# An attention-score kernel: transposes over other PSUM buffers, evacuation two to one, and another place for the second unit's transposes

## The chip, the core and the metric

The kernel runs on one core of one Trainium2 chip. The metric is the device time of one execution in microseconds. Three runs of the kernel before gave 202.73, 202.91 and 203.09; the median is 202.91.

## The reference

```
batch, heads, seq, dim = 8, 8, 512, 64          # q and k, float32
scale = 1.0 / np.sqrt(q.shape[-1])
out = (np.einsum('bhqd,bhkd->bhqk', q, k) * scale).astype(np.float32)
```

For each of 64 pairs of batch and head, a 512 by 64 matrix `q` is multiplied with the transpose of a `k` of the same size, and scaled by 1/8. There is no softmax. Inputs are 16.8 MB, the output is 67.1 MB.

## The kernel before, in words

**Units and tiles.** The eight batches are taken two at a time: four units (`v`). A unit's `k` and `q` are loaded as 128 partitions of 16 KB each, so a partition holds 64 consecutive rows of one head. A unit's output is written in four tiles (`t`), each of four heads of one batch: two pairs of heads (`x`), with eight rows (`i`) of 512 per partition. That is 128 by 8192 floats, 4 MiB, one DMA each. So there are 8 loads of 2 MiB and 16 stores of 4 MiB, all issued by SP, in one queue, in the order of the program.

**Buffers in SBUF.** `big_pool` has three buffers of 4 MiB, and both a unit's inputs and an output tile take one. Four units are loaded at the start of the program: units 0, 1 and 2 take the three buffers, unit 3 takes the first again as soon as unit 0 is cast. Output tile 0 takes the buffer of unit 1, tile 1 that of unit 2, tile 2 that of unit 3, tile 3 that of tile 0, and so on: a tile's buffer is free when the store three before it has landed.

**Casts.** `load_and_cast` (L73) turns each input into bf16 `xb` in two halves, on POOL (L82).

**Transposes.** `transpose` (L98) is a generator. TensorE transposes eight 128 by 128 blocks into one PSUM bank (`tp`, two buffers; L107 for `k`, L116 for `q`), and `rearrange` (L87) copies the bank to SBUF in four copies of 64 partitions (L95), into `kT` or into `qz`, which holds zeros between its halves. Whole tiles alternate between DVE and ACT by the counter `n_tp`. A unit has four such tiles of `k` and four of `q`, and each tile gives five steps of the generator: its transposes, then four copies.

**Scores and evacuation.** `scores` (L123) multiplies into `ps` (three buffers of two banks, L132) and `evacuate` (L60) scales 128 by 1024 floats from PSUM to the output tile: 8 per tile, 128 in all. Of each six, three are on ACT (L64) and three on DVE (L66).

**Order.** All of these are pinned to the program's order on their engine. Unit 0 is transposed at once. From then on the steps of the next unit's generator are taken between evacuations of the present unit (L158): one or two after each.

Of the kernel before, what the change touches and what calls it, by code (L numbers as in the profile page):

```python
# [1 line left out]

# [5 lines left out]


@with_exitstack  # L10
def kernel(
    ctx: ExitStack,
    tc: tile.TileContext,
    q: bass.AP,
    k: bass.AP,
    out: bass.AP,
):

    nc = tc.nc
    B, H, S, D = q.shape
    scale = 1.0 / (D ** 0.5)
    P = 128
    UNITS = B // 2
    N = H
    M = P // (2 * H)  # L30
    R = S // M
    J = R // 2
    RO = 8
    U = S // RO
    JJ = J // RO
    IW = 8 // JJ
    TILES = N // 2

    f32 = mybir.dt.float32
    bf16 = mybir.dt.bfloat16  # L40

    q_r = q.rearrange("(v b) g (m j) d -> v (b g m) (j d)", b=2, j=R)
    k_r = k.rearrange("(v b) g (m j) d -> v (b g m) (j d)", b=2, j=R)
    out_r = out.rearrange("(v b) (t x h) (u i) k -> v (b t) (h u) x (i k)", b=2, x=2, h=2, i=RO)

    consts = ctx.enter_context(tc.tile_pool(name="consts", bufs=1))

    big_pool = ctx.enter_context(tc.tile_pool(name="big", bufs=3))
    bf_pool = ctx.enter_context(tc.tile_pool(name="bf", bufs=6))
    t_pool = ctx.enter_context(tc.tile_pool(name="t", bufs=2))  # L50
    tpsum_pool = ctx.enter_context(tc.tile_pool(name="tpsum", bufs=2, space=bass.MemoryType.PSUM))
    psum_pool = ctx.enter_context(tc.tile_pool(name="psum", bufs=3, space=bass.MemoryType.PSUM))


    pinned = tc.keep_in_program_order

    n_evac = 0
    n_tp = 0

    def evacuate(dst, src):  # L60
        nonlocal n_evac

        if n_evac % 6 in (0, 2, 3):
            pinned(nc.scalar.mul(out=dst, in_=src, mul=scale))  # L64
        else:
            pinned(nc.vector.tensor_scalar(out=dst, in0=src, scalar1=scale, scalar2=None,  # L66
                                           op0=mybir.AluOpType.mult))
        n_evac += 1

    def half(h):  # L70
        return slice(h * D, (h + 1) * D)

    def load_and_cast(v):  # L73

        xf = big_pool.tile([P, 2, 2, J * D], f32, name="big")
        both = []
        for x, src in enumerate((k_r, q_r)):
            nc.sync.dma_start(out=xf[:, x], in_=src[v].rearrange("p (s c) -> p s c", s=2))  # L78
        for x in range(2):
            xb = bf_pool.tile([P, J, 2, D], bf16, name="xb")  # L80
            for s in range(2):
                pinned(nc.gpsimd.tensor_copy(out=xb[:, :, s, :],  # L82
                                             in_=xf[:, x, s].rearrange("p (j d) -> p j d", j=J)))
            both.append(xb)
        return both

    def rearrange(tp, pattern, dst):  # L87

        nonlocal n_tp
        copy = (nc.vector.tensor_copy, nc.scalar.copy)[n_tp % 2]  # L90
        n_tp += 1
        for s in range(2):
            src = tp[half(s)].rearrange(pattern, n=N, h=2)
            for h in range(2):
                pinned(copy(out=dst(s, h), in_=src[:, h]))  # L95
                yield

    def transpose(v, kb, qb):  # L98


        kT = t_pool.tile([P, N, M, 2, J], bf16, name="kT")
        qz = qzs[v % 2]
        ts[v] = (kT, qz)
        for j0 in range(0, J, 8):
            tp = tpsum_pool.tile([P, 8, P], bf16, name="tp")
            for j in range(8):
                pinned(nc.tensor.transpose(out=tp[:, j, :], identity=identity,  # L107
                                           in_=kb[:, j0 + j].rearrange("p s d -> p (s d)")))
            yield
            yield from rearrange(tp, "d j (n h m) -> d h n m j",  # L110
                                 lambda s, h: kT[half(h), :, :, s, j0:j0 + 8])
        for i0 in range(0, RO, IW):
            tp = tpsum_pool.tile([P, IW, JJ, P], bf16, name="tp")
            for i in range(IW):
                for jj in range(JJ):
                    pinned(nc.tensor.transpose(out=tp[:, i, jj, :], identity=identity,  # L116
                                               in_=qb[:, RO * jj + i0 + i].rearrange("p s d -> p (s d)")))
            yield
            yield from rearrange(tp, "d i jj (n h m) -> d h i n m jj",
                                 lambda s, h: qz[half(h), i0:i0 + IW, :, h * U:(h + 1) * U]  # L120
                                 .rearrange("d i n (m s jj) -> d s i n m jj", s=2, jj=JJ)[:, s])

    def scores(v, t):  # L123

        kT, qz = ts[v]
        o = big_pool.tile([P, 2, RO, S], f32, name="big")
        for x in range(2):
            n = 2 * t + x
            for i in range(0, RO, 2):
                ps = psum_pool.tile([P, 2, S], f32, name="ps")  # L130
                for w in range(2):
                    pinned(nc.tensor.matmul(out=ps[:, w, :], lhsT=qz[:, i + w, n, :],  # L132
                                            rhs=kT[:, n].rearrange("d m s j -> d (m s j)"),
                                            start=True, stop=True))
                evacuate(o[:, x, i:i + 2, :], ps)
                yield
        nc.sync.dma_start(out=out_r[v, t], in_=o.rearrange("p x i k -> p x (i k)"))  # L137

    def take(steps, count):
        for _ in range(count):  # L140
            next(steps, None)

    identity = consts.tile([P, P], dtype=bf16)
    make_identity(nc, identity)
    qzs = [consts.tile([P, RO, N, P], bf16, name=f"qz{n}") for n in range(2)]
    for qz in qzs:
        nc.vector.memset(qz, 0.0)  # L147
    cast = [load_and_cast(v) for v in range(UNITS)]

    ts = {}  # L150
    for _ in transpose(0, *cast[0]):
        pass
    for v in range(UNITS):
        ahead = transpose(v + 1, *cast[v + 1]) if v + 1 < UNITS else iter(())
        for t in range(TILES):
            for n, _ in enumerate(scores(v, t)):

                take(ahead, 1 + (t > 0 if v == 0 else n % 4 == 3))  # L158
        for _ in ahead:
            pass  # L160


# [1 line left out]
_INS = ['q', 'k']  # L164
_OUTS = [((8, 8, 512, 512), 'float32')]


# [23 lines left out]
```

## Time and profile before

| | |
|---|---|
| median of three runs | 202.91 us |
| the profiled execution | 203.03 us |
| its span, first to last instruction | 201.3 us |
| busy: PE, DVE, ACT, POOL | 99.2, 126.4, 100.7, 30.6 us |
| queue q1 (all loads and stores) | 83.89 MB, 98.1% of 16 engines |
| mean granted TensorE clock | 0.833 |

The span lies within the profiled execution's time, with 1.7 us around it. The page gives busy time by engine, then the span in 40 slices of 5.03 us with a digit for the busy tenths of each engine and of the DMA engines. A group of instructions is shown as busy time and mean duration, and then as the idle time of its engine just before them with what ended it. The windows view gives the same for stretches that one chooses, the timeline gives single instructions.

### The profile page before, as it was taken

How to read it: one execution, taken by the hardware profiler on the slowest of the kernel's cores; microseconds unless marked ns; L12 is line 12 of the kernel's file. 1: busy time of each engine (PE TensorE's matmuls, PEld its weight loads, DVE VectorE, ACT ScalarE, POOL GpSimd, SP SyncE). 2: the span in 40 equal slices, each digit the busy share in tenths (PEclk: the TensorE clock that was granted, in tenths of full speed). 3: DMA queues.
4: the chain of work that ended last, by engine and by line, in shares of the span. 5: the costliest groups of instructions: out<-in, count | busy, mean ns of one | idle time of the engine just before them, and what ended most of it. 6: DMA issues, size and time to landing. Idle time of an engine off the chain costs nothing.

```text
span 201.3 us, 1456 instructions
## 1 busy us (share of the span) xinstructions
PE 99.2 (49%) x503; PEld 48.3 (24%) x512; DVE 126.4 (63%) x130; ACT 100.7 (50%) x129; POOL 30.6 (15%) x22
## 2 busy tenths in 40 slices
PE   0033366753976729463729554856535666710000
PEld 0033353321522414231315221432212222200000
DVE  6726659995989929796749796569635264530000
ACT  2016667786674856583837663856515341510000
POOL 1277777556000000000000000000000000000000
PEclk9999999998599996999975998888995857555555
DMA  6999999999999999999999999999999999999993
GB/s 205 430 443 430 420 433 440 420 407 427 433 436 425 422 443 427 430 423 440 430 423 433 433 430 427 440 430 423 433 436 430 410 446 433 420 423 433 433 427 163
DMA packets 5510, 83.97 MB, mean 417 GB/s; under 512 B 384, under 2 KB 384, under 8 KB 384
## 3 DMA queue, kind: packets, MB, share of 16 engines
q1 hardware_dynamic: 5504, 83.89, 98.1%
q8 instruction: 4, 0.07, 0.1%
q14 instruction: 2, 0.02, 0.0%
HBM read 16.78 MB, written 67.11 MB: 417 GB/s over the span
## 4 chain that ended last, share of the span: by engine, by line
DMA 63%; DVE 16%; PE 3%; POOL 3%; ACT 1%; POOLq 1%; issue 1%; SPq 0%; DVEq 0%; ACTq 0%
DMA out_dram<-big 43%; DMA big<-in_q_dram 20%; DVE big L66 12%; PE ps L132 3%; DVE qz L95 3%; POOL xb L82 3%; DVE kT L95 1%; ACT big L64 1%; POOLq L186 1%; SPq L78 0%; DVEq L66 0%; SPq L137 0%; ACTq L64 0%; POOLq L82 0%
## 5 line engine op out<-in xcount | busy, mean ns | idle before, releaser
L132 PE MATMUL ps<-kT,qz 128*128 128x512 bf16 x247 | 81.1, 450 | 55.1 <-ACT big L64 39.2
L66 DVE TENSOR_SCALAR big<-ps 128x1024 f32<-128x1024 f32 x64 | 76.3, 1222 | 39.9 <-DMA out_dram<-big 29.1
L64 ACT ACTIVATE big<-ps 128x1024 f32<-128x1024 f32 x64 | 63.7, 1023 | 57.0 <-DMA out_dram<-big 30.8
L132 PEld LDWEIGHTS <-qz 128*128 128x128 bf16 x256 | 27.5, 111 | 96.0 <-issue 83.2
L82 POOL CAST xb<-big 128x2048 bf16<-128x2048 f32 x16 | 29.9, 1896 | 17.6 <-DMA big<-in_k_dram 11.9
L95 DVE COPY kT<-tp 64x512 bf16<-64x512 bf16 x32 | 22.0, 687 | 6.3 <-PE tp L107 5.7
L95 ACT COPY kT<-tp 64x512 bf16<-64x512 bf16 x32 | 18.5, 578 | 14.7 <-PE tp L107 14.4
L95 DVE COPY qz<-tp 64x512 bf16<-64x512 bf16 x32 | 22.0, 687 | 3.1 <-PE tp L116 2.7
L95 ACT COPY qz<-tp 64x512 bf16<-64x512 bf16 x32 | 18.5, 578 | 3.9 <-PE tp L116 3.6
L107 PE MATMUL tp<-identity,xb 128*128 128x128 bf16 x128 | 12.0, 254 | 16.5 <-POOL xb L82 12.5
L116 PE MATMUL tp<-identity,xb 128*128 128x128 bf16 x128 | 12.8, 265 | 6.0 <-DVE kT L95 3.5
L107 PEld LDWEIGHTS <-xb 128*128 128x128 bf16 x128 | 10.5, 116 | 20.8 <-POOL xb L82 12.8
L116 PEld LDWEIGHTS <-xb 128*128 128x128 bf16 x128 | 11.3, 122 | 10.9 <-issue 8.9
L147 DVE MEMSET qz<- 128x4096 uint32 x2 | 6.9, 3472 | 2.5 <-PEq L175 1.7
L95 ACT ACT_TABLE_LOAD x1 | 1.3, 1283 | 0.7 <-PEq L175 0.7
masks.py:199 POOL TENSOR_SCALAR_AFFINE_SELECT identity<-identity 128x128 bf16<-128x128 bf16 x1 | 0.3, 294 | 0.1
masks.py:197 POOL MEMSET identity<- 128x128 bf16 x1 | 0.2, 205 | 0.3 <-POOLq L175 0.3
L175 POOL MEMSET const-float32-0.0<- 128x1 f32 x1 | 0.1, 99 | 0.2 <-issue 0.2
L175 POOL MEMSET const-bfloat16-1.0<- 128x1 bf16 x1 | 0.1, 102 | 0.0
L175 POOL MEMSET const-uint8-127<- 128x1 uint8 x1 | 0.1, 102 | 0.0
L175 POOL MEMSET const-float32-1.0<- 128x1 f32 x1 | 0.1, 99 | 0.0
## 6 DMA issues: line engine op xcount, KB each, us to landing
out_dram<-big SPq DMA_DIRECT2D x16, 4096.0 KB, 21.4
big<-in_k_dram SPq DMA_DIRECT2D x4, 2048.0 KB, 19.2
big<-in_q_dram SPq DMA_DIRECT2D x4, 2048.0 KB, 24.2
```

Of the source, the lines that this page charges most:

```text
L64: pinned(nc.scalar.mul(out=dst, in_=src, mul=scale))
L66: pinned(nc.vector.tensor_scalar(out=dst, in0=src, scalar1=scale, scalar2=None, op0=mybir.AluOpType.mult))
L82: pinned(nc.gpsimd.tensor_copy(out=xb[:, :, s, :], in_=xf[:, x, s].rearrange("p (j d) -> p j d", j=J)))
L95: pinned(copy(out=dst(s, h), in_=src[:, h]))
L107: pinned(nc.tensor.transpose(out=tp[:, j, :], identity=identity, in_=kb[:, j0 + j].rearrange("p s d -> p (s d)")))
L116: pinned(nc.tensor.transpose(out=tp[:, i, jj, :], identity=identity, in_=qb[:, RO * jj + i0 + i].rearrange("p s d -> p (s d)")))
L132: pinned(nc.tensor.matmul(out=ps[:, w, :], lhsT=qz[:, i + w, n, :], rhs=kT[:, n].rearrange("d m s j -> d (m s j)"), start=True, stop=True))
L147: nc.vector.memset(qz, 0.0)
L175: nc = _bacc.Bacc("TRN2", target_bir_lowering=False, num_devices=1)
L186: with _tile.TileContext(nc) as tc:
```

## The change

Five things are done.

1. The first of unit 0's casts goes from POOL to DVE.
2. `tp` is one tile of two banks, allocated once. Unit 0's transposes use these two banks and two buffers of `ps` in turn, so that DVE and ACT each have two PSUM buffers.
3. For units 2 and 3 the two banks are taken as one: sixteen transposes, and four copies of 1024 elements where there were eight of 512.
4. Evacuations go to ACT, ACT, DVE in turn.
5. The steps of unit 1's generator are taken 0, 0, 3 and 2 after each evacuation in the tiles 0 to 3 of unit 0; those of units 2 and 3 (twenty each) after evacuations 0, 1, 3, 5 and 7 of each tile.

```
     def evacuate(dst, src):
...
-        if n_evac % 6 in (0, 2, 3):
+        if n_evac % 3 < 2:
             pinned(nc.scalar.mul(out=dst, in_=src, mul=scale))
...
-                pinned(nc.gpsimd.tensor_copy(out=xb[:, :, s, :],
-                                             in_=xf[:, x, s].rearrange("p (j d) -> p j d", j=J)))
+                copy = nc.vector.tensor_copy if v == x == s == 0 else nc.gpsimd.tensor_copy
+                pinned(copy(out=xb[:, :, s, :], in_=xf[:, x, s].rearrange("p (j d) -> p j d", j=J)))
...
-        for j0 in range(0, J, 8):
-            tp = tpsum_pool.tile([P, 8, P], bf16, name="tp")
-            for j in range(8):
-                pinned(nc.tensor.transpose(out=tp[:, j, :], identity=identity,
-                                           in_=kb[:, j0 + j].rearrange("p s d -> p (s d)")))
+        W = 8 if v < 2 else 16
+
+        def transposed(rows):
+            if v == 0 and n_tp % 4 > 1:
+                tp = psum_pool.tile([P, W, P], bf16, name="ps")
+            elif v < 2:
+                tp = tps[:, n_tp % 2]
+            else:
+                tp = tps.rearrange("p b w c -> p (b w) c")
+            for w, row in enumerate(rows):
+                pinned(nc.tensor.transpose(out=tp[:, w, :], identity=identity,
+                                           in_=row.rearrange("p s d -> p (s d)")))
+            return tp
+
+        for j0 in range(0, J, W):
+            tp = transposed([kb[:, j0 + j] for j in range(W)])
             yield
             yield from rearrange(tp, "d j (n h m) -> d h n m j",
-                                 lambda s, h: kT[half(h), :, :, s, j0:j0 + 8])
+                                 lambda s, h: kT[half(h), :, :, s, j0:j0 + W])
+        IW = W // JJ
         for i0 in range(0, RO, IW):
...
+            tp = transposed([qb[:, RO * jj + i0 + i] for i in range(IW) for jj in range(JJ)])
             yield
...
+    tps = tpsum_pool.tile([P, 2, 8, P], bf16, name="tp")
...
-                take(ahead, 1 + (t > 0 if v == 0 else n % 4 == 3))
+                take(ahead, (0, 0, 3, 2)[t] if v == 0 else n == 0 or n % 2)
```

## The prediction

> **What bounds the kernel now.** The slices of the page come first, because one row there is full from end to end. Then the queue's row, and the stretch after the loads.
>
> ```profile
> DMA  6999999999999999999999999999999999999993
> q1 hardware_dynamic: 5504, 83.89, 98.1%
> 44.00:195.00 151.00, 81.63 (x374) 36.23 (x378) 95.31 (x98) 78.70 (x98) 3.74 (x2) 0.80 1.01 430
> ```
>
> The third line is a stretch of the windows view: length, busy time of PE, PEld, DVE, ACT and POOL, granted clock, DMA share, GB/s. The transfers are the only thing with no gaps: 83.89 MB at 430 GB/s is 195 us, and with a start (first issue at 0.74 us) and an end it is the span of 201.3. No compute engine passes 63%. So the question is only: does the one DMA queue ever run empty, now or after? Next I read when stores are issued (timeline of SP, one window each) and when a buffer comes back.
>
> ```profile
> 38.23 0.40 SPq L137 DMA_DIRECT2D out_dram<-big  x1
> 46.05 0.39 SPq L137 DMA_DIRECT2D out_dram<-big  x1
> 58.31 0.37 SPq L137 DMA_DIRECT2D out_dram<-big  x1
> 63.61 0.37 SPq L137 DMA_DIRECT2D out_dram<-big  x1
> ...
> 83.93 2.86 ACT L64 ACTIVATE big<-ps 128x1024 f32<-128x1024 f32 x3 [2.48 <-DMA out_dram<-big]
> ...
> 93.64 1.94 ACT L64 ACTIVATE big<-ps 128x1024 f32<-128x1024 f32 x2 [3.36 <-DMA out_dram<-big]
> ```
>
> Buffers return 9.71 us apart (93.64 - 83.93): one 4 MiB store. Counting back from 83.82, where the chain of waits has the landing of the store issued at 63.61, the stores land at 54.7, 64.4, 74.1 and 83.8. In the trace's landing records the first of the 16 DMA engines is done 2.3 to 2.7 us before the last: about 52.0, 61.7, 71.3, 81.0. A store must be issued before those times, less the start-up of a transfer (first issue at 0.74, first packets from 1.75: I take 1.3 us). The spare time of the first four issues is 4 us (loads end at 42.3 on the first engine), 5.9, 3.4 and 7.7. The queue never empties, and the third store is the tight one.
>
> ```profile
> L66 DVE TENSOR_SCALAR big<-ps 128x1024 f32<-128x1024 f32 x64 | 76.3, 1222 | 39.9 <-DMA out_dram<-big 29.1
> L64 ACT ACTIVATE big<-ps 128x1024 f32<-128x1024 f32 x64 | 63.7, 1023 | 57.0 <-DMA out_dram<-big 30.8
> L82 POOL CAST xb<-big 128x2048 bf16<-128x2048 f32 x16 | 29.9, 1896 | 17.6 <-DMA big<-in_k_dram 11.9
> L95 DVE COPY kT<-tp 64x512 bf16<-64x512 bf16 x32 | 22.0, 687 | 6.3 <-PE tp L107 5.7
> L95 ACT COPY kT<-tp 64x512 bf16<-64x512 bf16 x32 | 18.5, 578 | 14.7 <-PE tp L107 14.4
> ```
>
> Both evacuating engines wait mostly for DMA; they are ahead of it. These durations are my prices.
>
> **What the Trainium skill says.** "DMA: Bandwidth & Descriptors", section "Queues, rings and completion order": each DMA engine takes its descriptors in ring order. The trace agrees: landings in issue order, 9.71 us apart. So a store issued earlier does not move ahead of the loads, nor slow them. Same page, "Where 436 GB/s comes from": a fabric ceiling of 435 GB/s; the trace has 430, so no rate is left to win. "VectorE: DVE Perf Modes", section on the TRN2 errata: from PSUM, DVE costs 120 cycles plus one per element at 0.96 GHz, ScalarE 172 plus one at 1.2 GHz. For 512 elements an estimate of 0.66 and 0.57 us; the trace has 0.69 and 0.58. "SBUF — State Buffer", section "Who interferes with whom": a DVE copy in a 2-port mode and GpSimd block each other for a whole instruction. No overlap of that kind is in the trace.
>
> **The change, part by part.** The sum is against the profiled execution: span 201.3, 203.03 us in all, 0.06% above the median of 202.91.
>
> Cast on DVE: one POOL cast of 1.90 us goes, one DVE cast comes. Bounds: 1.2 us (page's 2-port copy, 2048 elements) to 2.3 us (one element per cycle). DVE is free from 9.40 (after two memsets of 3.47); blocked by POOL's own cast (8.71 to 10.6) it ends at 11.8 to 12.9, against 12.4 before. The next loads wait for all four casts of unit 0, the last of which ends at 17.3 because q lands at 13.5: unmoved. Worth 0, and a loss is hidden too, since six loads keep the queue filled to 33 us.
>
> First transposes on four PSUM buffers: PE no longer waits for copies (2.1 to 2.4 us, three times in unit 0). q is cast at 17.3; its four tiles of eight transposes take 3.7 us (16 in 1.87); DVE then has two tiles of 4 x 0.69: ready at about 24 instead of 29.4. But evacuation of tile 0 needs unit 1's load buffer, whose casts end at 27.1. With no interleaved steps and six ACT evacuations of 0.93 to 1.02, store 0 is issued at about 33 (38.23 before), and store 1, which waits for unit 2's casts at 36.9, at about 42.3 (46.05). These 4 to 5 us are real and worth nothing: the loads fill the queue to 42.3.
>
> Second unit's copies moved into tiles 2 and 3 (40 steps: 3 and 2 per evacuation). Tile 2 waits for unit 3's casts at 48.8, as before. ACT then has 5 evacuations and 8 copies ahead of the last one: 5 x 1.02 + 8 x 0.58 = 9.7, DVE 3 x 1.22 + 6 x 0.69 = 7.8 (two copies run during the wait). Store 2: 58.6 (58.31 before). Tile 3 begins there: 6 x 1.02 + 6 x 0.58 = 9.6, store 3 at 68.0 (63.61 before). Spare time: 3.1 and 3.3 us, against 1.3 needed. Covered, but it is the thinnest cover in the kernel.
>
> Later units: 64 copies of 512 elements on both engines become 32 of 1024. Price: the 1024-element evacuation from PSUM, 1.22 and 1.02 us (page: 1.19 and 1.00); bounds 1.0 to 1.4. Evacuations go two to ACT, one to DVE. Per unit ACT has 21.3 x 1.02 + 8 x 1.02 = 29.9 us (before 16 x 1.02 + 16 x 0.58 = 25.6), DVE 10.7 x 1.22 + 8 x 1.22 = 22.8 (before 30.5). The fuller engine is at 30 us in both, against 4 x 9.71 = 38.8 of transfers. The busiest tile (ACT copies, t of 1 and 3) costs ACT 5.33 x 1.02 + 4 x 1.02 = 9.5 us, just under 9.71. Both banks of the transposed tile are one buffer now, so 16 transposes wait for the copies of the last 16, and PE's score matmuls queue behind them; ACT and DVE wait for those. Laying the instructions end to end with these prices and the clock granted before, the spare times of stores 4 to 15 are 2.0 us (store 9) to 10 (near the end). Never empty.
>
> SP: the same 24 DMAs in the same order, none moved past another. The sum: 0.
>
> **The rivals.** *The queue starves (slower).* Place: stores 2, 3 and 7 to 9. Spare time there is 2 to 3.3 us where 1.3 is needed. The trace's clock was 0.80 after 44 us, with spells at half; 16 transposes take 0.9 us at full and 1.7 at half clock. A spell over a heavy tile costs about 1 us of spare. It decides where a store comes later than 1.3 us before its first engine runs out; and the last engine, which sets the end, has another 2.3 us, so a lost sum up to about 2.3 is still free. With spells over most heavy tiles 3 to 4.5 us are lost, 0.7 to 2.2 beyond that: 203.6 to 205.1. Against it: total PE work is unchanged, so I see no reason for more half-clock time.
>
> *The tail of the slowest DMA engine moves.* The last store lands between 198.1 and 200.4; each collision with an instruction fetch put its engine back by about 1 us (packets of 0.9 to 1.1 us instead of 0.61 stand beside each of the four fetches on q8). Other timing may spare or add one: 202.0 to 203.9. A gain needs both late engines (0.1 us apart at the end) to be spared; a loss only one hit.
>
> *The front counts (faster).* If something other than transfers held the stores, store 0's 5 us would come through: 197.7. Against: DMA share 0.99 to 1.01 from 2.5 to 195 us. I give it 0.02. That the order is not as described is out: the built instruction order shows it.
>
> **How the numbers follow.** No change that can be told (0.2%, 0.41 us, is about what a measurement of this kernel can tell): 0.67, at 202.9. Starved 0.17 and a longer tail 0.08: slower 0.25. A shorter tail 0.06 and the front 0.02: faster 0.08. Range 202.2 (most of a spared tail) to 204.5 (half of the starved case); the likeliest case alone holds 202.5 to 203.3.
>
> **What would show it.** Store 0 issued at 33, store 1 at 42.3, store 2 at 58 to 59.5, store 3 at 67.5 to 69; a DMA row of nines throughout; wide copies at 1.22 and 1.02; ACT busier than DVE (by the prices, about 124 to 101 us). A slice with a DMA digit under 9 after the first would be starvation, and the store issued last before it names the tile. A time under 202.4 with the row unchanged would mean that the tail moved.

## The result and the profile after

The changed kernel takes 227.98 us (median of four runs, 227.07 to 228.71) beside 203.0 of the kernel before: a ratio of 1.123, 95% interval 1.118 to 1.127. The forecast was no change, 202.9 us, with a range up to 204.5. It was wrong by 25 us. Ratios leave out executions well above a kernel's fastest, so for some kernels below they are less than the quotient of the medians, and where the two differ the ratio is the one to compare.

The same rows of the page are read first: the DMA slices (5.66 us each now), and the queue's row.

```profile
DMA  7999999999804922989999898979898999999995
q1 hardware_dynamic: 5504, 83.89, 87.8%
```

The row of nines has a hole: from the eleventh slice on it reads 8, 0, 4, 9, 2, 2. The same 83.89 MB filled 98.1% of the span before and fill 87.8% of a longer one. Now the stretches of the windows view (length, PE, PEld, DVE, ACT, POOL, granted clock, DMA share, GB/s).

```profile
60.00:95.00 35.00, 19.15 (x85) 10.33 (x87) 14.85 (x18) 16.87 (x23) 0.00 (x0) 0.50 0.50 211
95.00:170.00 75.00, 44.60 (x223) 22.57 (x225) 41.84 (x35) 50.45 (x52) 0.00 (x0) 0.84 0.93 396
```

Half of 35 us is lost in the first stretch, 17.5 us, and 7% of 75, 5.2 us, in the second. In the first no engine is at work for much more than half of the time: DVE 42%, ACT 48%, PE 55% at half clock. So they wait for each other. The issues of the first four stores, in the timeline of SP, say where.

```profile
36.21 0.40 SPq L146 DMA_DIRECT2D out_dram<-big  x1
41.96 0.39 SPq L146 DMA_DIRECT2D out_dram<-big  x1
70.22 0.37 SPq L146 DMA_DIRECT2D out_dram<-big  x1
88.42 0.37 SPq L146 DMA_DIRECT2D out_dram<-big  x1
```

Stores 0 and 1 come earlier than before (38.23, 46.05), as forecast, though store 0 only at 36.21 where 33 was forecast. Stores 2 and 3, forecast at 58.6 and 68.0, come at 70.22 and 88.42. These are the two tiles among whose evacuations unit 1 is transposed. The waits view names what holds them (who waited for whom: us in total, times, longest).

```profile
DVE big L65 <- PE ps L141: 50.7, 28, 6.9
...
PE tp L114 <- DVE kT L94: 20.0, 5, 8.7
...
PE tp L114 <- DVE qz L94: 13.9, 5, 3.3
...
PE tp L114 <- ACT kT L94: 13.2, 5, 3.5
...
PE tp L114 <- ACT qz L94: 7.8, 3, 3.0
```

TensorE waits 54.9 us for copies (the four rows of `tp` together) before it may transpose, in all units. Of the kernel before the page shows 6.0 and 16.5 us of idle time ahead of all transposes, most of the latter for the first cast:

```profile
L107 PE MATMUL tp<-identity,xb 128*128 128x128 bf16 x128 | 12.0, 254 | 16.5 <-POOL xb L82 12.5
L116 PE MATMUL tp<-identity,xb 128*128 128x128 bf16 x128 | 12.8, 265 | 6.0 <-DVE kT L95 3.5
```

What such a wait looks like is seen in two rounds of tile 2, in the timeline of the changed kernel (weight loads and score matmuls are left out).

```profile
57.46 0.77 PE L114 MATMUL tp<-identity,xb 128*128 128x128 bf16 x8 [3.54 <-ACT kT L94]
...
58.34 0.68 DVE L94 COPY kT<-tp 64x512 bf16<-64x512 bf16 x1 [7.18 <-PE tp L114]
59.12 1.22 DVE L65 TENSOR_SCALAR big<-ps 128x1024 f32<-128x1024 f32 x1
...
59.98 1.02 ACT L63 ACTIVATE big<-ps 128x1024 f32<-128x1024 f32 x1 [2.56 <-PE ps L141]
60.36 2.10 DVE L94 COPY kT<-tp 64x512 bf16<-64x512 bf16 x3
62.51 1.01 PE L114 MATMUL tp<-identity,xb 128*128 128x128 bf16 x8 [2.58 <-DVE kT L94]
...
63.56 1.17 ACT L94 COPY kT<-tp 64x512 bf16<-64x512 bf16 x2 [2.56 <-PE tp L114]
64.75 1.02 ACT L63 ACTIVATE big<-ps 128x1024 f32<-128x1024 f32 x1
65.80 1.18 ACT L94 COPY kT<-tp 64x512 bf16<-64x512 bf16 x2
67.03 1.01 PE L114 MATMUL tp<-identity,xb 128*128 128x128 bf16 x8 [2.65 <-ACT kT L94]
```

Eight transposes, four copies with an evacuation among them on DVE, and only then (62.46 to 62.51) the next eight transposes, which go to the other bank; then the same on ACT. In all of unit 1 DVE and ACT never copy at the same time; only evacuations of the one run beside work of the other, as at 59.98. The two banks behave as one buffer. A round, from one group's transposes to the next group's, takes 4.5 to 6.3 us. The eight rounds of unit 1, the first of them half done, stand between 48.5, where unit 3's cast ends and tile 2's buffer is free, and store 3.

The theory after this reading (A): `tps` is one tile, and its banks are released together, that is, neither may be written again before both have been copied out. Transposes into one bank wait for the copies out of the other, score matmuls queue behind those transposes on PE, and the evacuating engines wait for the scores. Rivals: the place of unit 1's steps in tiles 2 and 3 is the cost (B), evacuation two to one makes ACT the bound (C), or the wide tiles of units 2 and 3 do it.

### The profile page after: what moved, and what is told of

Its sections match the earlier page's. It is cut to its first block, busy times and chain, and to the rows that moved or that the text cites. A ratio compares the mean times of both kernels' runs of the same rounds, so it can differ in the third digit from the quotient of the medians.

```text
span 226.2 us, 1413 instructions
## 1 busy us (share of the span) xinstructions
PE 106.5 (47%) x503; PEld 53.2 (24%) x512; DVE 100.9 (45%) x93; ACT 119.3 (53%) x135; POOL 30.6 (14%) x21
## 3 DMA queue, kind: packets, MB, share of 16 engines
q1 hardware_dynamic: 5504, 83.89, 87.8%
## 5 line engine op out<-in xcount | busy, mean ns | idle before, releaser
L63 ACT ACTIVATE big<-ps 128x1024 f32<-128x1024 f32 x86 | 84.2, 1025 | 55.3 <-PE ps L141 21.9
L65 DVE TENSOR_SCALAR big<-ps 128x1024 f32<-128x1024 f32 x42 | 51.4, 1225 | 68.5 <-PE ps L141 50.7
L114 PEld LDWEIGHTS <-xb 128*128 128x128 bf16 x256 | 25.3, 135 | 76.0 <-issue 62.5
L94 DVE COPY kT<-tp 64x512 bf16<-64x512 bf16 (+1 forms) x20 | 18.0, 901 | 14.2 <-PE tp L114 13.9
L94 DVE COPY qz<-tp 64x512 bf16<-64x512 bf16 (+1 forms) x20 | 18.0, 902 | 11.5 <-PE tp L114 11.1
L94 ACT COPY qz<-tp 64x512 bf16<-64x512 bf16 (+1 forms) x20 | 15.0, 749 | 6.6 <-PE tp L114 6.4
L94 ACT COPY kT<-tp 64x512 bf16<-64x512 bf16 (+1 forms) x20 | 15.0, 749 | 5.6 <-PE tp L114 5.3
L114 PE MATMUL ps<-identity,xb 128*128 128x128 bf16 x32 | 3.8, 311 | 0.0
L94 DVE COPY kT<-ps 64x512 bf16<-64x512 bf16 x4 | 2.8, 689 | 2.0 <-PE ps L114 2.0
L94 DVE COPY qz<-ps 64x512 bf16<-64x512 bf16 x4 | 2.8, 688 | 2.0 <-PE ps L114 2.0
```

What stands on the lines that cost most here:

```text
L114: pinned(nc.tensor.transpose(out=tp[:, w, :], identity=identity, in_=row.rearrange("p s d -> p (s d)")))
```

## The experiments

**Two tiles in place of one.** The pool has two tiles of one bank. Units 2 and 3 stay at eight transposes, and their steps are taken where the kernel before takes them.

```
-            elif v < 2:
-                tp = tps[:, n_tp % 2]
             else:
-                tp = tps.rearrange("p b w c -> p (b w) c")
+                tp = tpsum_pool.tile([P, W, P], bf16, name="tp")     # pool: bufs=2; W = 8; steps 1 + (n % 4 == 3)
```

> The changed kernel, but each group of eight transposes gets a tile of its own from a pool of two (and units 2 and 3 stay at eight transposes[...]); casts, two-to-one evacuation and the place of unit 1's steps are kept. Theory A (the two banks of one allocated tile are released together, so transposes into one bank wait for the copies out of the other): the waits of transposes for copies in unit 1 go, store 2 is issued near 58.8 and store 3 near 69.4, the queue does not empty, 202.7 to 204.5 us. Theory B (the bunching of unit 1's steps in tiles 2 and 3 is the cost): store 3 stays later than 80 us, 212 us or more. Theory C (two-to-one evacuation makes ACT the bound): above 210 us with DMA digits under 9 in the later units.

Measured: 203.28 us, ratio to the kernel before 1.0015 (1.0008 to 1.0021). The DMA row of its page:

```profile
DMA  6999999999999999999999999999999999999993
```

Stores 2 and 3 in its timeline of SP:

```profile
58.58 0.37 SPq L144 DMA_DIRECT2D out_dram<-big  x1
67.30 0.37 SPq L144 DMA_DIRECT2D out_dram<-big  x1
```

The hole is gone, with casts, evacuation split and place of the steps as in the change. B and C fall: where the transposed tiles are two, both together cost some 0.3 us. In its timeline two copies by ACT run beside three by DVE, and transposes wait 5.1 us for copies in all.

```profile
53.97 2.10 DVE L94 COPY kT<-tp 64x512 bf16<-64x512 bf16 x3
54.51 1.16 ACT L94 COPY kT<-tp 64x512 bf16<-64x512 bf16 x2
```

**Two tiles first, wide ones later.** This one keeps the wide tile for units 2 and 3: the pool of two is closed after unit 1, and one of two banks opened.

```
+        if v == 1:
+            narrow.close()
+            wide.append(ctx.enter_context(tc.tile_pool(name="wide", bufs=1, space=bass.MemoryType.PSUM)))
```

> The changed kernel with two tiles of its own for units 0 and 1, and one tile of two banks for units 2 and 3 as in the change (the small pool is closed and a wide one opened in its place). It tells the wide tiles of units 2 and 3 apart from the shared tile of unit 1. Theory A: stores 2 and 3 as in the two-tile kernel; the wide tiles have a single buffer, so 16 transposes wait for the last 16's copies: between no loss (clock as in the kernel before) and 5 us (clock as in the changed kernel): 203 to 208 us. If the wide tiles were the cause of the 25 us: 215 us or more. If they are free: within 0.5 us of the two-tile kernel.

Measured: 206.88 us, ratio 1.015 (1.011 to 1.019). Its DMA row has no hole, but from the 24th slice of 5.13 us (118 us) to the 30th it falls below nine three times:

```profile
DMA  6999999999999999999999989799989999999994
```

So wide tiles in units 2 and 3, with their steps at other places, cost some 3 us against two tiles of eight (ratios 1.015 and 1.0015). The wide tile is a single buffer by design: 16 transposes wait for the copies of the 16 before (PE waits 25.9 us for copies in all here). The rest of the 25 us, 227.98 - 206.88 = 21 us, belongs to the tile that units 0 and 1 share, since all else is as in the changed kernel.

**The shared tile alone.** The kernel before, with this edit and nothing else:

```
-            tp = tpsum_pool.tile([P, 8, P], bf16, name="tp")
+            tp = tps[:, n_tp % 2]          # tps: one tile of two banks, allocated once; the same for q
```

> The kernel before, with one edit: its two transposed tiles become the two banks of one tile that is allocated once; order, casts, evacuation split and eight transposes at a time stay. Theory A: every group of transposes waits for the copies of the group before, with the score matmuls queued behind it on PE; store 0 near 53 us, store 3 near 91 us, the queue empty several times, 229 to 238 us, with TensorE at half clock for more of the time than before. Theories B and C (place of the steps, evacuation split): neither is in this kernel, so 202.5 to 204 us.

Measured: 238.46 us, ratio 1.176 (1.171 to 1.180), just above A's range. Stores 0 and 3 are issued at 53.63 and 90.03 us, where A had them, and PE waits 69.4 us for copies. Its DMA row empties in unit 1 and dips all through the later units, since here they share the tile too:

```profile
DMA  7999999008729479999999696899695799999995
```

The edit changes only how the tile is allocated and named: the order of instructions is pinned as before, and two banks are used as before. It costs 35 us. B and C expected nothing from it.

**The place of the steps.** The changed kernel with unit 1's steps where the kernel before has them.

```
-                take(ahead, (0, 0, 3, 2)[t] if v == 0 else n == 0 or n % 2)
+                take(ahead, 1 + (t > 0) if v == 0 else n == 0 or n % 2)
```

> The changed kernel with unit 1's steps taken where the kernel before takes them (one after each evacuation of tile 0, two in tiles 1 to 3), all else as changed, the shared tile too. Theory A with the place as a multiplier: each wait for copies now falls also into tiles 0 and 1, where the loads still fill the queue, so part of the loss is hidden: store 1 near 54, store 3 near 77, 207 to 212 us. Theory B: 202.5 to 204 us. If the place has no part in it: 225 us or more.

Measured: 210.04 us, ratio 1.035 (1.030 to 1.041). Stores 1 and 3 are issued at 52.55 and 73.85 us. The shared tile is there, and 18 us of its cost are not: part of the rounds falls into tiles 0 and 1, where the loads still fill the queue. So the place is harmless with two tiles and costs 18 us with one. It is a multiplier and not a cause.

**The half clock.** TensorE was granted 0.50 from 60 to 95 us. Is that part of the loss? The test needs a PSUM bank that nothing else uses, so its control has two score buffers:

```
-    psum_pool = ctx.enter_context(tc.tile_pool(name="psum", bufs=3, space=bass.MemoryType.PSUM))
+    psum_pool = ctx.enter_context(tc.tile_pool(name="psum", bufs=2, space=bass.MemoryType.PSUM))
```

> The changed kernel with two score buffers in PSUM where it has three (ps), which frees two banks. It is the control for the next kernel. Theory A: the copies hold the transposes, not the score buffers, so stores 2 and 3 stay near 70 and 88 us; 227 to 231 us. If the score buffers were what is short: 235 us or more.

Measured: 226.72 us, ratio 1.104 (1.096 to 1.113), with stores 2 and 3 at 68.73 and 86.52. The score buffers are not what is short. The test proper puts extra matmuls where PE waits:

```
+            for _ in range(4 if v > 0 else 0):
+                pinned(nc.tensor.matmul(out=warm, lhsT=identity, rhs=kb[:, 0:4].rearrange("p j s d -> p (j s d)"),
+                                        start=True, stop=True))
             for w, row in enumerate(rows):
```

> As the control, with four 128x512 matmuls into one of the freed banks ahead of each group of transposes of units 1 to 3; nothing reads that bank. On PE they stand where PE waits for copies. Theory A1 (PE's waits let its clock fall to half, and the half clock lengthens each round of transposes, copies, score matmuls): TensorE stays at full clock between 50 and 95 us, store 3 comes several us before the control's, 8 to 12 us less than the control in all: 217 to 222 us. Theory A2 (the clock is a symptom that costs nothing, or does not follow PE's work): the four matmuls add to PE's queue, same as the control or up to 4 us more.

Measured: 221.99 us, ratio 1.088 (1.081 to 1.096); the clock from 60 to 95 us rose to 0.89, from 0.70 in the control. But store 3 is issued at 86.29 us, against 86.52 in the control. By the ratios some 3 us are gained, with intervals that just overlap; A1 expected 8 to 12, and a store 3 several us earlier. To find where, the extra matmuls were put in unit 1 alone and in the later units alone, beside the control again.

> Two score buffers and the four extra matmuls ahead of each group of transposes, in unit 1 alone (the stretch from 48 to 90 us, where the queue is empty longest). The kernel with them in units 1 to 3 had the higher clock there and yet the same store 3 as its control. If the clock works in the later units only: same as the control within 1.5 us, about 225 us. If it works in unit 1: store 3 below 85 us and 3 us or more less than the control.

> The same extra matmuls in units 2 and 3 alone, whose wide tiles have a single buffer and 16 transposes in a group (0.9 us at full clock, 1.8 at half). If the clock works there: DMA digits under 9 after 95 us become fewer, 3 to 5 us less than the control: 219 to 222 us. If the gain of the first such kernel was the scatter of these runs: same as the control within 1.5 us.

> The control once more, beside the two others on one chip and with more rounds: the changed kernel with two score buffers, 223 to 228 us. Its own executions should be shorter where their mean clock is higher, if the clock has a part in the time.

Measured, in this order: 223.88 us, ratio 1.091 (1.086 to 1.096); 221.40 us, 1.090 (1.086 to 1.093); control 223.87 us, 1.101 (1.097 to 1.105). By the ratios the extra matmuls gain about 2.0 us in unit 1 and 2.3 us in the later units, with intervals just clear of the control's: each more than the 1.5 that stood for no effect and less than the 3 that stood for one. The stretch from 60 to 95 us in the windows view, with the extra matmuls in unit 1:

```profile
60.00:95.00 35.00, 19.71 (x107) 9.86 (x109) 17.33 (x19) 18.87 (x24) 0.00 (x0) 0.90 0.61 257
```

The same stretch in the control beside it:

```profile
60.00:95.00 35.00, 19.06 (x89) 9.42 (x91) 15.57 (x18) 17.86 (x23) 0.00 (x0) 0.61 0.57 240
```

The clock goes from 0.61 to 0.90 and the DMA share only from 0.57 to 0.61, which is 1.4 us of 35; store 3 comes at 84.52 instead of 85.84 (the profiled executions took 224.80 and 222.96 us). So the half clock is not what emptied the queue: most of a round is copies and evacuations on DVE and ACT, and PE's eight transposes are 1.0 us of its 4.5 to 6.3. Whether the 2.3 us in the later units come by the clock is not settled: in single profiles of that stretch the clock is 0.93 with them and 0.94 and 0.80 in the two of the control. Over the ten executions of the control, on two chips, the three with the highest mean clock (0.833 to 0.844) had spans of 220.6 to 221.1 us, the others, at 0.785 to 0.816, 221.4 to 226.7. A lower clock goes with a longer run, by a few us; which of them is the cause stays open. "TensorE: Matmul & The Clock Gate", Part 1 of the Trainium skill, says that the throttled state is the default and that activity releases it; the traces agree, since from 60 to 84 us, where only unit 1 is transposed, PE was granted 0.86 and 0.93 in the two kernels with extra matmuls there, and 0.50 to 0.71 in the changed kernel and the three others without them.

## Why the prediction was wrong

**What failed: the step of unit 1's copies ("Store 2: 58.6", "store 3 at 68.0"), and with it "First transposes on four PSUM buffers: PE no longer waits".** Both took the two banks of `tps`, whose index alternates, for two buffers. They are one tile. For the later units the prediction said so itself ("Both banks of the transposed tile are one buffer now"), and it did not ask whether that held for units 0 and 1. In the trace each of the seven groups of transposes of unit 1 after the first waits for copies by DVE and ACT in turn, 25.3 us together. In unit 0 PE still waits three times (2.9, 1.0 and 2.9 us), so DVE and ACT did not have two PSUM buffers each, as the change meant them to; the copies end at 29.67 us, no earlier than before, where about 24 was forecast and two tiles give 24.64. That part cost nothing, since the loads filled the queue meanwhile.

**The size of it, by the prediction's own terms.** Tile 2 had ACT at 9.7 us and DVE at 7.8, and the larger was taken, since the engines work side by side. With one buffer they mostly take turns, and each group's transposes stand between: 9.7 + 7.8 + 4 x 1.0 = 21.5, from the cast at 48.5 to 70.0. Measured: 70.22. A maximum became a sum. This sum was made afterwards, and that it fits so closely is in part luck: two of ACT's evacuations (48.52 and 59.98) ran beside DVE's work, which takes 2.0 us off, and waits that the sum leaves out, for score matmuls mostly, put about as much on. Tile 3 took another 18.2 us where 9.6 were reckoned (by which store 3 would be at 68.2; the 68.0 is a slip).

**The spare time was right and far too small for that.** The first DMA engine ran out at 61.7 us; a store issued at 70.22 leaves about 9.8 us empty with the 1.3 of start-up, and the next, 18.2 us later against 9.7 of transfer, another 8.5. That is 18 of the 25 us. The landings agree: store 3 lands at 101.6 us (13.2 after its issue), and with two tiles at 83.1.

**The rival "the queue starves" had the right place and sign** (stores 2, 3 and the later units) at 0.17, and the wrong mechanism: half-clock spells, worth 0.7 to 2.2 us. The statement "I see no reason for more half-clock time" was wrong too: the mean clock fell from 0.833 to 0.779. How much of the 25 us goes with that is open; the runs above found 2 to 3 us where the extra matmuls were put in.

**"Never empty" for the wide tiles was wrong**: some 3 us were lost, where 2.0 us of spare were reckoned for the tightest store. The price of a copy was right, as this row of the groups of the changed kernel shows for DVE; ACT's is 1005 ns. What was short was the cover; which wait used it up was not followed store by store.

```profile
L94 DVE COPY qz<-tp 64x1024 bf16<-64x1024 bf16 x8 | 9.8, 1222 | 8.9 <-PE tp L114 8.7
```

**What held.** The cast on DVE moved nothing, but not as the prediction had it. It took 1.16 us (1.2 to 2.3 were allowed) and was not held up by POOL's cast; POOL's cast beside it took 3.78 us, where one takes about 1.9, and 3.6 to 3.8 in every other run with this edit. So the first transposes began at 12.28 us, against 12.50 before. The first line is of the kernel before (two casts), the others are of the changed one.

```profile
8.71 3.73 POOL L82 CAST xb<-big 128x2048 bf16<-128x2048 f32 x2 [7.41 <-DMA big<-in_k_dram]
...
8.45 3.78 POOL L82 CAST xb<-big 128x2048 bf16<-128x2048 f32 x1 [7.15 <-DMA big<-in_k_dram]
9.32 1.16 DVE L82 CAST xb<-big 128x2048 bf16<-128x2048 f32 x1
```

The front's gain was real with two tiles and worth nothing: store 0 comes at 33.61 us (33 forecast), store 1 at 43.55 (42.3), and the time is within 0.3 us of the kernel before. Evacuation two to one costs no more than that. With two tiles stores 2 and 3 are at 58.58 and 67.30, against 58.6 and 68.0: the working fits the kernel that it assumed, which was not the one that was built.

No version here beats the kernel before. Moving less data, or starting the queue earlier, was not tried.

## What to carry to other kernels

Count the buffers by what is allocated and released, not by indices: a tile that is sliced into two banks may be one buffer to everything that waits, and two engines that take turns on it cost nearly the sum of their work instead of the larger part. Look for a producer that waits alternately for its two consumers, as PE does here. In a kernel that is bound by transfers the spare time of each store is the number to know. Here the 5 us by which store 0 came earlier with two tiles were worth nothing, and the loss beyond the spare time came through whole: store 3 landed 18.5 us later than with two tiles, and the end came 25 us later.

## What the runs showed of the hardware

The clock granted to TensorE was higher where PE had more to do: four 128x512 matmuls ahead of each group of transposes went with 0.90 in place of 0.61 in a stretch whose DMA share went only from 0.57 to 0.61. A cast of 128x2048 elements on POOL took 3.78 us with one on DVE beside it, and about 1.9 without. And the kernel whose queue runs empty scatters more: 222.4 to 228.5 us over six runs of the control, where 203.1 to 203.7 are the ends of twenty runs of the kernel with two tiles.
